# A hybrid transformer step on one core: attention logits as three rounded products, and heads 4 to 7 turned at other places

## The chip, the core and the metric

The kernel runs on one core of a Trainium2 chip. The metric is the device time of one execution in microseconds (us); lower is better. Several engines work beside one another, each on its own list of instructions: TensorE (PE) multiplies matrices, VectorE (DVE) and ScalarE (ACT) do elementwise work, GpSimd (POOL) and SyncE (SP) mostly issue transfers. They wait for one another by semaphores.

## The reference

One sequence of 512 tokens goes through a state-space layer with a convolutional feed-forward layer, and an attention layer with a second feed-forward layer, all in float32. The change touches only the logits of the attention, and what prepares them. Cut to that:

```python
k, v = kv[..., :K_DIM].reshape(b, s, 8, 2, 64), kv[..., K_DIM:].reshape(b, s, 8, 128)
k = rms_norm(k, k_norm_g)                       # over the 64 of each map
q = rms_norm((rms_norm(x, ln_g) @ q_w).reshape(b, s, 8, 2, 64), q_norm_g)
logits = einsum('bqhcd,bkhcd->bhcqk', q, k) * 64 ** -0.5 + rel_bias[t5_bucket(dist)]
p = softmax(where(dist >= 0, logits, -inf))     # causal; c = 0, 1 are the two maps of a head
attn = p[:, :, 0] - lam * p[:, :, 1]
o = einsum('bhqk,bkhd->bqhd', attn, v)
x = x + (rms_norm(o, subln_g) * (1 - lam_init)).reshape(b, s, -1) @ out_w
```

There are 8 heads, each with two maps of 64 dimensions; the result of a head is the difference of the two maps' softmaxes times the values.

## The kernel before, in words

Tokens lie in NT = 4 blocks of 128. Large products (projections) are taken as three float32r ("rounded") products: each operand is split into a rounded high part and a rounded rest, and high x high, high x low and low x high are added up in a PSUM bank. The helpers write the rounded high part on ACT (`wh_`, `xgh`, `oh`) and the rest on DVE (`wl_`, `xgl`, `ol`).

**Keys and queries.** `qk("q0")` projects the queries of heads 0 to 3, `keys` all keys by a seven-product scheme (the sums named `ps_K`), while `qk("q1")` (queries of heads 4 to 7) is part of the filling work described below. `head_norm` normalises each map (DVE, L1361) and `turned` turns blocks of 128 x 128 with transposes on TensorE into a PSUM bank, four to a bank; ACT (L1375) copies a bank with the gain into `kT[0]`, `kT[1]`, `qT[0]` and `qT[1]`, float32 tiles of 128 rows (two maps of 64) x 4 heads x 512 tokens. The sums of the second keys (heads 4 to 7) are kept in `qT[1]`, which is not needed yet. Unturned raw sums of the key scheme lie in a tile `key_raw` of the pool `kc`, which is closed when the keys are done; the pool `units` then takes over its memory.

**Attention lines.** Each head is cut into three units by `PARTS`: the query blocks 0 and 1, block 2, block 3, so that a unit has 384, 384 or 512 key columns a map (blocks 0 and 1 have 128 and 256). For a unit `logits` (L1527) multiplies the two maps side by side, rows 0 to 63 and rows 64 to 127 of the tiles, into two PSUM banks; DVE adds the bias `tb` and takes the maximum (L1533), ACT takes the exponential (L1540), DVE weighs the two maps (L1550: `weigh`), TensorE turns the result (L1559, step `a`), ACT copies it (L1560), TensorE multiplies it with the values (L1570, step `v`), and a finished head is normalised and turned for the output projection (step `o`, L1592, split by L1596 and L1597). The bias tile `tb` of a head is loaded by SP in the first unit of the head (two buffers); its first memory lies in the pool `units`.

TensorE's instructions in this part run in the order of the program text, which is written by hand in `ORDER`: 12 lines that each begin with a step `L` (the logits of two units, that is, one of (0, 1), (2, next head's 0) or (1, 2)) and one line more. `f` is one step of filling work: a part of a projection of six matmuls (values `v0`, queries `q1`, values `v1`, then the output projection). The instructions of the other engines and the transfers are put in order by the framework's scheduler. PSUM has four banks for turned, logits and value tiles (`aux_bank`) and four for projections, each taken in rotation.

Of the kernel before, what the change touches and what calls it, by code (L numbers as in the profile page):

```python
# [18 lines left out]
P = 128  # L19
T = 512  # L20
# [22 lines left out]
def trunk_kernel(ctx: ExitStack, tc, x, ssm_ln_g, ssm_in_w, ssm_conv_w, ssm_conv_b, ssm_dt_bias,  # L43
# [1249 lines left out]
    with tc.tile_pool(name="att", bufs=1) as ap, ExitStack() as later:  # L1293
        rts = []
        late = []

        kT = [ap.tile([P, 4, T], F32, name="kT%d" % i) for i in range(2)]
        qT = [ap.tile([P, 4, T], F32, name="qT%d" % i) for i in range(2)]
        vt = [ap.tile([P, D], F32, name="vt%d" % b) for b in range(NT)]

        def key_load(t, j, i, c, **more):
# [51 lines left out]
            act.activation(s, t, AF.Square)  # L1353
            dve.reduce_sum(out[:, b, :], s.rearrange("p (a q) -> p a q", a=8), axis=AX.X)

        def head_norm(key, kn, ss, dst, gcol, where):
            rsqrt_act(ss, ap, key, [P, NT, 8], 64)
            def normed():
                for b in range(NT):
                    v = kn[b].rearrange("p (a q) -> p a q", a=8)  # L1360
                    dve.tensor_tensor(out=v, in0=v, in1=ss[:, b, :].unsqueeze(2).to_broadcast([P, 8, 64]),  # L1361
                                      op=ALU.mult)

            if key == "q1":
                late.append(((0, 3), normed))
            else:
                normed()

            def turned(bs):
                for b in bs:  # L1370
                    ps = aux_bank("kt%s_%d" % (key, b))
                    for h in range(4):
                        pe.transpose(ps[:, h * P:(h + 1) * P], kn[b][:, h * P:(h + 1) * P], ident)
                    v = ps.rearrange("p (h t) -> p h t", h=4)
                    act.activation(dst[:, :, b * P:(b + 1) * P], v if key[0] == "k" else v[:, :, ::-1],  # L1375
                                   AF.Copy, scale=c2[:, gcol:gcol + 1])

            for at, bs in zip(where, ((0, 1), (2, 3))):
                late.append((at, lambda bs=bs: turned(bs)))

        def head_sums(key):
            return ap.tile([P, NT, 8], F32, tag="qss", name="ss" + key, bufs=2)

        def qk(key, dst, gcol, where):
            kn, ss = [], head_sums(key)

            def evac(b, ps, rt):
                t = ap.tile([P, T], F32, tag="kn", name="kn%s_%d" % (key, b), bufs=4)
                act.activation(t, ps, AF.Copy, scale=rt[:, b:b + 1])
                squared(key, t, rt, ss, b)  # L1390
                kn.append(t)

            yield from proj(key, evac)
            head_norm(key, kn, ss, dst, gcol, where)

        def keys(kc):

# [2 lines left out]

            def first(i, b, ps):
                acc[i][b] = (ap.tile([P, T], F32, tag="kn", name="key%d_%d" % (i, b), bufs=4) if i
                             else qT[1][:, b, :])
                if ps is not None:
                    act.activation(acc[i][b], ps, AF.Copy)

# [23 lines left out]
            def finish(i, where):  # L1430
                key, ss = "k%d" % (1 - i), head_sums("k%d" % (1 - i))
                for b in range(NT):
                    act.activation(acc[i][b], acc[i][b], AF.Copy, scale=rts[0][:, b:b + 1])
                    squared(key, acc[i][b], rts[0], ss, b)
                head_norm(key, acc[i], ss, kT[1 - i], 48, where)

            for m in SEVEN[1]:
                pss = [(aux_bank if m in "127" else mm_bank)("ps_K%s_%d" % (m, b)) for b in range(2)]
# [34 lines left out]
                        add(acc[0][2 + b], ps, r_)  # L1473
                if m == "3":
                    finish(1, ((4, 0), (4, 2)))
            finish(0, ((0, 1), (0, 3)))

        def vproj(key, i):
            def evac(b, ps, rt):
# [3 lines left out]
        PARTS = ((0, 1), (2,), (3,))  # L1483
        ORDER = ("f f L f f f a f",
# [12 lines left out]
        fl = lambda a: a.rearrange("p a b -> p (a b)")  # L1497
# [1 line left out]
        class Unit:  # L1499
# [9 lines left out]
            def logits(self):  # L1509
                h, tag, st = self.h, self.tag, self.st  # L1510
                if self.part == 0:
                    st["tb"] = up.tile([P, T], F32, tag="tb", name="tb%d" % h, bufs=2)
                    sync.dma_start(st["tb"], bass.AP(tensor=bd.tensor, offset=h * NBIAS + 1, ap=[[1, P], [1, T]]))
                    st["sm"] = up.tile([P, NT, 2], F32, tag="sm", name="sm%d" % h, bufs=3)
                i2, h4 = h // 4, h % 4
                k = len(self.ii)
                mx = up.tile([P, k, 2], F32, tag="mx%d" % k, name="mx" + tag, bufs=3)
                self.sm = st["sm"][:, self.ii[0]:self.ii[-1] + 1, :]
                self.p = [up.tile([P, T], F32, tag="p%d" % m, name="lg%s_%d" % (tag, m), bufs=3)
                          for m in range(2)]  # L1520
                pss = [aux_bank("lg%s_%d" % (tag, m)) for m in range(2)]
                for j, i in enumerate(self.ii):
                    n = (i + 1) * P
                    c = slice(self.off[j], self.off[j] + n)
                    for m in range(2):
                        rows = slice(64 * m, 64 * (m + 1))
                        pe.matmul(pss[m][:, c], qT[i2][rows, h4, i * P:(i + 1) * P], kT[i2][rows, h4, :n],  # L1527
                                  start=True, stop=True)
                for j, i in enumerate(self.ii):
                    n = (i + 1) * P  # L1530
                    c = slice(self.off[j], self.off[j] + n)
                    for m in range(2):
                        dve.tensor_tensor_reduce(self.p[m][:, c], pss[m][:, c],  # L1533
                                                 st["tb"][:, (3 - i) * P:], 1.0, 3.0e38,
                                                 ALU.add, ALU.min, mx[:, j, m:m + 1])
                for j, i in enumerate(self.ii):
                    n = (i + 1) * P
                    for m in range(2):
                        v = self.p[m][:, self.off[j]:self.off[j] + n]
                        act.activation(v, v, AF.Exp, bias=mx[:, j, m:m + 1], scale=-1.0,  # L1540
                                       accum_out=self.sm[:, j, m:m + 1])
# [103 lines left out]
            run(rest)  # L1645

        with tc.manual_schedule(engines={mybir.EngineType.PE}):
            run(qk("q0", qT[0], 49, (("2", 1), ("5", 0))))
            with tc.tile_pool(name="keys", bufs=1) as kc:
                keys(kc)  # L1650
            op_ = later.enter_context(tc.tile_pool(name="att_o", bufs=1))
            up = later.enter_context(tc.tile_pool(name="units", bufs=1))
            fill = chain(vproj("v0", 0), qk("q1", qT[1], 49, ((2, 0), (2, 1))), vproj("v1", 1),
                         attn_out(0, None, range(KB)))
            us = []
            for h in range(AH):
                st = {}
                us += [Unit(h, part, st) for part in range(len(PARTS))]
            for _ in range(10):
                next(fill)  # L1660

            turned, valued = iter(us), iter(us)
            valued_heads, normed_heads = [], []

            def norm_heads():
                while valued_heads:
                    u = valued_heads.pop(0)
                    normed_out(u.h, u.st)
                    normed_heads.append(u)

            def values():
                u = next(valued)
                u.values()
                if u.part == len(PARTS) - 1:
                    valued_heads.append(u)
                    if os:
                        with tc.issue_after(state["ol"]):
                            norm_heads()
                    norm_heads()

            def head_out():
                u = normed_heads.pop(0)
                os.append(turned_out(u.h, u.st))

            steps = {"f": lambda: next(fill), "a": lambda: next(turned).turn(), "v": values, "o": head_out}
            pairs = iter(zip(us[::2], us[1::2]))
            for step in " ".join(ORDER).split():
                if step == "L":
                    pair = next(pairs)
                    for u in pair:  # L1690
                        u.logits()
                    for u in pair:
                        u.weigh()
                else:
                    steps[step]()
            assert next(fill, None) is None
            last_out(norm1)
# [38 lines left out]
```

## Time and profile before

| | us |
|---|---|
| median of 3 runs | 1317.28 (1316.26 to 1317.30) |
| the profiled execution, its own time | 1317.05 |
| its span | 1315.3 |
| keys, in the span | about 745 to 808 |
| attention lines 0 to 11 and the line behind | about 808 to 945 |

The granted clock was full throughout. Times in the profile's rows are microseconds from the start of the span; PE is TensorE's matmuls, PEld its loads of the stationary operand, SPq and POOLq are transfers as they are issued. Matmuls are pipelined: the duration of one includes the way through the array, and what it costs is the distance from its start to the next one's. A group "x12" counts instructions of the trace; a float32 matmul stands there as two, a rounded one as one.

### The profile page before, as it was taken

The page shows a single profiled execution, that of the slowest core. Times are in us where ns is not written, and L with a number is a line of the kernel's source. Part 1 is how long each engine was busy: PE and PEld are TensorE (multiplying, and loading weights), DVE is VectorE, ACT ScalarE, POOL GpSimd, SP SyncE. Part 2 cuts the span into 40 slices and gives each one's busy share as a digit, 9 for nine tenths or more (in the row PEclk, how much of TensorE's full clock was granted, in tenths as well). Part 3 has the DMA queues.
Part 4 walks back from the last instruction along what each step waited for, and adds up shares of the span by engine and source line. Part 5 has one row for each costly group of instructions (what it writes and reads, how often), then busy time and mean ns, then how long its engine had stood idle before and what let it go on. Part 6 is the DMA issues. An engine that isn't in the chain of part 4 may idle for free.

```text
span 1315.3 us, 18265 instructions
## 1 busy us (share of the span) xinstructions
PE 1307.8 (99%) x6771; PEld 1096.2 (83%) x6771; DVE 1073.1 (82%) x1774; ACT 713.8 (54%) x1156; POOL 176.8 (13%) x244
## 2 busy tenths in 40 slices
PE   9999999999999999999999999999999999999998
PEld 8878888888888988898889887777888888888887
DVE  7989878888888877876888878677777978887886
ACT  6696554743344445544556667676654444544452
POOL 5230200300021401020113210000020100010001
PEclk9999999999999999999999999999999999999999
DMA  7453433432234657673766754222224445443635
GB/s 210 150 162 88 150 101 109 138 95 87 82 96 138 124 142 203 180 161 113 216 168 145 192 128 120 73 65 66 64 80 160 98 118 186 103 96 112 192 64 128
DMA packets 202552, 167.84 MB, mean 128 GB/s; under 512 B 7580, under 2 KB 175904, under 8 KB 202464
## 3 DMA queue, kind: packets, MB, share of 16 engines
q1 hardware_dynamic: 176080, 124.93, 31.8%
q0 software_dynamic: 22928, 36.46, 14.7%
q10 hardware_dynamic: 3456, 5.30, 1.1%
q8 instruction: 53, 0.87, 0.3%
q14 instruction: 35, 0.29, 0.1%
HBM read 160.21 MB, written 6.44 MB: 127 GB/s over the span
## 4 chain that ended last, share of the span: by engine, by line
PE 98%; ACT 1%; DVE 1%; issue 0%; DVEq 0%
PE ps_g L209 6%; PE ps_u L210 6%; PE ps_g L210 6%; PE ps_u L209 6%; PE ps_u L208 6%; PE ps_g L208 6%; PE ps_in L208 5%; PE ps_in L210 5%; PE ps_in L209 5%; PE ps_s L1239 3%; PE ps_s L1244 3%; PE ps_s L1242 3%; PE ps_s L1146 3%; PE ps_s L1141 3%; PE ps_s L1144 3%; PE ps_o L209 2%
## 5 line engine op out<-in xcount | busy, mean ns | idle before, releaser
L208 PE MATMUL ps_u<-xgh,wh_u 128*128 128x512 f32 x352 | 137.4, 390 | 0.0
L209 PE MATMUL ps_g<-xgl,wh_g 128*128 128x512 f32 x352 | 137.2, 390 | 0.0
L208 PE MATMUL ps_g<-xgh,wh_g 128*128 128x512 f32 x352 | 137.0, 389 | 0.0
L210 PE MATMUL ps_u<-xgh,wl_u 128*128 128x512 f32 x352 | 137.0, 389 | 0.0
L210 PE MATMUL ps_g<-xgh,wl_g 128*128 128x512 f32 x352 | 137.0, 389 | 0.0
L209 PE MATMUL ps_u<-xgl,wh_u 128*128 128x512 f32 x352 | 136.9, 389 | 0.0
L208 PE MATMUL ps_in<-xgh,wh_in 128*128 128x512 f32 x304 | 122.9, 404 | 0.0
L210 PE MATMUL ps_in<-xgh,wl_in 128*128 128x512 f32 x304 | 119.7, 394 | 0.0
L209 PE MATMUL ps_in<-xgl,wh_in 128*128 128x512 f32 x304 | 119.2, 392 | 0.0
L209 PEld LDWEIGHTS ps_g<-xgl,wh_g 128*128 128x128 f32 x352 | 66.0, 188 | 14.3 <-DVE xgl L488 0.7
L1244 PE MATMUL ps_s<-sl,wh_s 128*128 128x256 f32 x308 | 77.5, 283 | 0.0
L1242 PE MATMUL ps_s<-sh,wh_s 128*128 128x256 f32 x308 | 77.5, 283 | 0.0
L210 PEld LDWEIGHTS ps_g<-xgh,wl_g 128*128 128x128 f32 x352 | 66.1, 188 | 13.7
L209 PEld LDWEIGHTS ps_u<-xgl,wh_u 128*128 128x128 f32 x352 | 66.1, 188 | 13.6
L210 PEld LDWEIGHTS ps_u<-xgh,wl_u 128*128 128x128 f32 x352 | 66.0, 188 | 13.7
L208 PEld LDWEIGHTS ps_g<-xgh,wh_g 128*128 128x128 f32 x352 | 66.1, 188 | 13.6
L208 PEld LDWEIGHTS ps_u<-xgh,wh_u 128*128 128x128 f32 x352 | 66.1, 188 | 13.6
L1126 ACT ACTIVATE sh<-vg 128x256 fp32r<-128x256 f32 (+1 forms) x44 | 23.1, 524 | 99.1 <-DVE vg L1276 99.1
L1052 POOL DMA_DIRECT2D wz<-in_ffn_down_w_dram x36 | 44.2, 1290 | 235.2 <-DVE wl_s L1080 163.1
L1272 ACT ACTIVATE vg<-vg 128x512 f32<-128x512 f32 x44 | 27.8, 632 | 78.4 <-DVE vg L1024 78.3
L1024 DVE SCALAR_TENSOR_TENSOR vg<-ug,cf,vg 128x511 f32<-128x511 f32 x88 | 65.8, 747 | 5.5 <-ACT vg L1022 4.1
L1024 DVE SCALAR_TENSOR_TENSOR vu<-uu,cf,vu 128x511 f32<-128x511 f32 x88 | 65.7, 747 | 2.8 <-ACT vu L1022 1.4
(425 smaller groups left out, 3465.0 us busy)
## 6 DMA issues: line engine op xcount, KB each, us to landing
wr_g<-in_ffn_up_w_dram SPq DMA_DIRECT2D x44, 512.0 KB, 3.9
wr_u<-in_ffn_up_w_dram SPq DMA_DIRECT2D x44, 512.0 KB, 3.9
wr_in<-in_ssm_in_w_dram SPq DMA_DIRECT2D x40, 512.0 KB, 3.9
wz<-in_ffn_down_w_dram POOLq DMA_DIRECT2D x27, 512.0 KB, 5.8
m<-cumd POOLq DMA_DIRECT2D x16, 512.0 KB, 4.7
wr_out<-in_ssm_out_w_dram SPq DMA_DIRECT2D x16, 512.0 KB, 3.5
wr_s<-in_ffn_down_w_dram SPq DMA_DIRECT2D x13, 512.0 KB, 3.9
xT<-in_ffn_down_w_dram SPq DMA_DIRECT2D x10, 512.0 KB, 7.2
```

Of the source, the lines that this page charges most:

```text
L208: pe.matmul(ps, wh, xh, start=start, stop=False)
L209: pe.matmul(ps, wh, xl, start=False, stop=False)
L210: return pe.matmul(ps, wl, xh, start=False, stop=stop).ins
L1024: dve.scalar_tensor_tensor(out=v[:, s:], in0=u[:, :T - s], scalar=col(2 - s), in1=v[:, s:], op0=ALU.mult, op1=ALU.add)
L1052: pool.dma_start(view(t, nq), source(p0, c, nq, j, i), accum_op=ALU.add)
L1141: pe.matmul(pss[b], h, ws[q][1][:, cols], start=False, stop=end and q == qs[-1], skip_group_check=more)
L1144: pe.matmul(pss[b], h, ws[q][0][:, cols], start=first and q == qs[0], stop=False, skip_group_check=more)
L1146: pe.matmul(pss[b], w, ws[q][0][:, cols], start=False, stop=False, skip_group_check=more)
L1239: pe.matmul(v[:, b], wl[:, q, cols], h, start=False, stop=q == nq - 1, skip_group_check=not opens or b > 0)
L1242: pe.matmul(v[:, b], wh[:, q, cols], h, start=opens and q + b == 0, stop=False, skip_group_check=not opens or b > 0)
L1244: pe.matmul(v[:, b], wh[:, q, cols], w, start=False, stop=False, skip_group_check=not opens or b > 0)
L1272: act.activation(ga, ga, AF.Silu)
```

## The change: what it does

The turned keys and queries are kept as a rounded high part and a rounded rest (`kT_hi`, `kT_lo`, `qT_hi`, `qT_lo`, room for four heads, so that heads 4 to 7 take the places of 0 to 3 when those are used up), and the logits of a map are three rounded products in place of one float32 product. `turn_head` turns one head into a bank; ACT writes the high part and DVE (a new operation, L1366 of the changed kernel) the rest, from the same bank. The heads 4 to 7 are turned by steps of their own in `ORDER` (`k4` to `k7`, `q4` to `q7`); before, all keys were turned within the key products and the `q1` projection, and the later queries in two pieces of the filling work. The sums of the second keys are kept in `key_raw`, and normalised into the right halves of the value tiles `vt`, which are free until the values of heads 4 to 7 are ready. In lines 4, 7 and 10 of `ORDER` (line 0 is the first) steps `v`, `o` and `f` are exchanged beside that.

```diff
-        kT = [ap.tile([P, 4, T], F32, name="kT%d" % i) for i in range(2)]
-        qT = [ap.tile([P, 4, T], F32, name="qT%d" % i) for i in range(2)]
+        turned_by = {n: [ap.tile([P, 4, T], F32R, name=n + "T_" + x) for x in ("hi", "lo")] for n in "kq"}
+        second = {}
...
+        def turn_head(kind, h, src):
+            ps = aux_bank("kt%s%d" % (kind, h))
+            for b in range(NT):
+                pe.transpose(ps[:, b * P:(b + 1) * P], src[b][:, h % 4 * P:(h % 4 + 1) * P], ident)
...
+            act.activation(hi, v, AF.Copy, scale=g)
+            dve.scalar_tensor_tensor(out=lo, in0=v, scalar=g, in1=hi.bitcast(F32), op0=ALU.mult, op1=ALU.subtract)
...
-                             else qT[1][:, b, :])
+                             else whole_sums[:, b // 2, 2 * (b % 2):2 * (b % 2) + 2].rearrange("p k t -> p (k t)"))
...
-                head_norm(key, acc[i], ss, kT[1 - i], 48, where)
+                head_norm(key, acc[i], ss, where, None if i else [v[:, T:] for v in vt])
...
         ORDER = ("f f L f f f a f",
                  "L f f a v f v f a f",
-                 "L f f a v f v f a f",
-                 "L f f a v f v f o a f",
-                 "L f f a v f v f o a f",
-                 "L f f a v f v a f",
-                 "L f f a v f v o a f",
-                 "L f f a f v f o a f",
-                 "L f f v a f v v a",
+                 "L f f k4 a v f v f a f",
+                 "L f f k5 a v f v f o a f",
+                 "L f f a v f f v o k6 a f",
+                 "L f f a v f q4 v a f",
+                 "L f f k7 a v f q5 v o a f",
+                 "L f f a f o q6 f v a f",
+                 "L f f q7 v a f v v a",
                  "L f f a v f v o a f",
-                 "L f f a v f v o a",
+                 "L f f a v o f v a",
                  "L f f a v f v a",
                  "f a v f o v")
...
-                    for m in range(2):
-                        rows = slice(64 * m, 64 * (m + 1))
-                        pe.matmul(pss[m][:, c], qT[i2][rows, h4, i * P:(i + 1) * P], kT[i2][rows, h4, :n],
-                                  start=True, stop=True)
+                    for z, (q, k) in enumerate(((qh, kh), (ql, kh), (qh, kl))):
+                        for m in range(2):
+                            rows = slice(64 * m, 64 * (m + 1))
+                            pe.matmul(pss[m][:, c], q[rows, h4, i * P:(i + 1) * P], k[rows, h4, :n],
+                                      start=z == 0, stop=z == 2)
```

Three places show it in the order of instructions. First TensorE in line 0, the logits of the first unit (`lg0_0_0` and `lg0_0_1` are the banks of its two maps). Before:

```order
L1527 MATMUL lg0_0_0_7622<-kT0_6903,qT0_6905 128x128
L1527 MATMUL lg0_0_1_7623<-kT0_6903,qT0_6905 128x128
L1527 MATMUL lg0_0_0_7622<-kT0_6903,qT0_6905 128x256
L1527 MATMUL lg0_0_1_7623<-kT0_6903,qT0_6905 128x256
L1527 MATMUL lg0_1_0_7639<-kT0_6903,qT0_6905 128x384
L1527 MATMUL lg0_1_1_7640<-kT0_6903,qT0_6905 128x384
```

and in the changed kernel, of which the first 10 of 18 rows are shown:

```order
L1536 MATMUL lg0_0_0_7630<-kT_hi_6903,qT_hi_6905 128x128
L1536 MATMUL lg0_0_1_7631<-kT_hi_6903,qT_hi_6905 128x128
L1536 MATMUL lg0_0_0_7630<-kT_hi_6903,qT_lo_6906 128x128
L1536 MATMUL lg0_0_1_7631<-kT_hi_6903,qT_lo_6906 128x128
L1536 MATMUL lg0_0_0_7630<-kT_lo_6904,qT_hi_6905 128x128
L1536 MATMUL lg0_0_1_7631<-kT_lo_6904,qT_hi_6905 128x128
L1536 MATMUL lg0_0_0_7630<-kT_hi_6903,qT_hi_6905 128x256
L1536 MATMUL lg0_0_1_7631<-kT_hi_6903,qT_hi_6905 128x256
L1536 MATMUL lg0_0_0_7630<-kT_hi_6903,qT_lo_6906 128x256
L1536 MATMUL lg0_0_1_7631<-kT_hi_6903,qT_lo_6906 128x256
```

Each product of a map became three, and the maps still alternate.

Second, SP's queue ahead of line 0, where `tb` is a bias tile and `wr_q`, `wr_v` are pieces of weights. Before:

```order
L140 DMA wr_q_0_7560<-in_q_w_dram 128x2x512
L1513 DMA tb_7616<-bd 128x512
L1513 DMA tb_7707<-bd 128x512
L140 DMA wr_q_2_7654<-in_q_w_dram 128x2x512
L140 DMA wr_q_4_7739<-in_q_w_dram 128x2x512
L140 DMA wr_q_6_7819<-in_q_w_dram 128x2x512
L140 DMA wr_v_0_7912<-in_kv_w_dram 128x2x512
```

In the changed kernel:

```order
L140 DMA wr_q_0_7564<-in_q_w_dram 128x2x512
L140 DMA wr_q_2_7674<-in_q_w_dram 128x2x512
L140 DMA wr_q_4_7771<-in_q_w_dram 128x2x512
L140 DMA wr_q_6_7827<-in_q_w_dram 128x2x512
L1520 DMA tb_7624<-bd 128x512
L1520 DMA tb_7731<-bd 128x512
L140 DMA wr_v_0_7935<-in_kv_w_dram 128x2x512
```

The first two bias loads moved behind three weight loads, and the first of them now waits for DVE's last operation on `key_raw` (the normalising of `vt3`).

Third, DVE ahead of line 0's first operation that reads a bias tile, the last row of each. Before:

```order
L174 SCALAR_TENSOR_TENSOR wl_q1_0_7563<-wr_q1_0_7560,c2_89,wh_q1_0_7562 128x512
L501 TENSOR_TENSOR rst_k1_7474<-ssk1_7456 128x32
L502 SCALAR_TENSOR_TENSOR rst_k1_7474<-rst_k1_7474,rsm_k1_7473 128x32
L503 SCALAR_TENSOR_TENSOR ssk1_7456<-rst_k1_7474,ssk1_7456 128x32
L1361 TENSOR_TENSOR qT1_6906<-qT1_6906,ssk1_7456 128x512 x4
L174 SCALAR_TENSOR_TENSOR wl_q1_2_7657<-wr_q1_2_7654,c2_89,wh_q1_2_7656 128x512
L1533 ISA lg0_0_0_7620,mx0_0_7619<-lg0_0_0_7622,tb0_7616 128x128
```

In the changed kernel, where `ktk0` to `ktk3` are the banks of the turned keys of heads 0 to 3:

```order
L501 TENSOR_TENSOR rst_k1_7478<-ssk1_7460 128x32
L1366 SCALAR_TENSOR_TENSOR kT_lo_6904<-ktk1_7585,c2_89,kT_hi_6903 128x512
L502 SCALAR_TENSOR_TENSOR rst_k1_7478<-rst_k1_7478,rsm_k1_7477 128x32
L503 SCALAR_TENSOR_TENSOR ssk1_7460<-rst_k1_7478,ssk1_7460 128x32
L1375 TENSOR_TENSOR vt0_6907<-key_raw_7106,ssk1_7460 128x512
L1375 TENSOR_TENSOR vt1_6908<-key_raw_7106,ssk1_7460 128x512
L1375 TENSOR_TENSOR vt2_6909<-key_raw_7106,ssk1_7460 128x512
L1375 TENSOR_TENSOR vt3_6910<-key_raw_7106,ssk1_7460 128x512
L1366 SCALAR_TENSOR_TENSOR kT_lo_6904<-ktk2_7604,c2_89,kT_hi_6903 128x512
L1366 SCALAR_TENSOR_TENSOR kT_lo_6904<-ktk3_7611,c2_89,kT_hi_6903 128x512
L174 SCALAR_TENSOR_TENSOR wl_q1_2_7677<-wr_q1_2_7674,c2_89,wh_q1_2_7676 128x512 x2
L1542 ISA lg0_0_0_7628,mx0_0_7627<-lg0_0_0_7630,tb0_7624 128x128
```

Low halves (L1366) of four heads came in (that of `ktk0` stands in the row above the first one shown), two of them ahead of the normalising, which now goes from `key_raw` to `vt`.

More of the change, by code (lines that the diff above doesn't have):

```diff
@@ L1354, in squared, with head_norm @@
             dve.reduce_sum(out[:, b, :], s.rearrange("p (a q) -> p a q", a=8), axis=AX.X)
-        def head_norm(key, kn, ss, dst, gcol, where):
+        def turn_head(kind, h, src):
+            ps = aux_bank("kt%s%d" % (kind, h))
+            for b in range(NT):
+                pe.transpose(ps[:, b * P:(b + 1) * P], src[b][:, h % 4 * P:(h % 4 + 1) * P], ident)
+            g = c2[:, 48:49] if kind == "k" else c2[:, 49:50]
+            v, hi, lo = (t.rearrange("p (b t) -> p b t", b=NT) for t in [ps] + [t[:, h % 4] for t in turned_by[kind]])
+            if kind == "q":
+                v = v[:, :, ::-1]
+            act.activation(hi, v, AF.Copy, scale=g)
+            dve.scalar_tensor_tensor(out=lo, in0=v, scalar=g, in1=hi.bitcast(F32), op0=ALU.mult, op1=ALU.subtract)
+        def head_norm(key, kn, ss, where, to=None):
             rsqrt_act(ss, ap, key, [P, NT, 8], 64)
+            to = to or kn
             def normed():
                 for b in range(NT):
-                    v = kn[b].rearrange("p (a q) -> p a q", a=8)
-                    dve.tensor_tensor(out=v, in0=v, in1=ss[:, b, :].unsqueeze(2).to_broadcast([P, 8, 64]),
+                    v, o = (t[b].rearrange("p (a q) -> p a q", a=8) for t in (kn, to))
+                    dve.tensor_tensor(out=o, in0=v, in1=ss[:, b, :].unsqueeze(2).to_broadcast([P, 8, 64]),
                                       op=ALU.mult)
@@ L1367, in head_norm, with qk @@
                 normed()
[L1369 to L1379, printed above, removed]
+            if key[1] == "1":
+                second[key[0]] = to
+                return
+            for at, hs in zip(where, ((0, 1), (2, 3))):
+                late.append((at, lambda hs=hs: [turn_head(key[0], h, to) for h in hs]))
         def head_sums(key):
             return ap.tile([P, NT, 8], F32, tag="qss", name="ss" + key, bufs=2)
-        def qk(key, dst, gcol, where):
+        def qk(key, where=()):
             kn, ss = [], head_sums(key)
@@ L1393, in qk @@
             yield from proj(key, evac)
-            head_norm(key, kn, ss, dst, gcol, where)
+            head_norm(key, kn, ss, where)
         def keys(kc):
@@ L1475, in keys @@
                     finish(1, ((4, 0), (4, 2)))
-            finish(0, ((0, 1), (0, 3)))
+            finish(0, ())
         def vproj(key, i):
@@ L1514, in logits @@
                     st["sm"] = up.tile([P, NT, 2], F32, tag="sm", name="sm%d" % h, bufs=3)
-                i2, h4 = h // 4, h % 4
+                (kh, kl), (qh, ql) = (turned_by[n] for n in "kq")
+                h4 = h % 4
                 k = len(self.ii)
@@ L1647, in trunk_kernel @@
         with tc.manual_schedule(engines={mybir.EngineType.PE}):
-            run(qk("q0", qT[0], 49, (("2", 1), ("5", 0))))
+            run(qk("q0", (("2", 1), ("5", 0))))
             with tc.tile_pool(name="keys", bufs=1) as kc:
@@ L1652, in trunk_kernel @@
             up = later.enter_context(tc.tile_pool(name="units", bufs=1))
-            fill = chain(vproj("v0", 0), qk("q1", qT[1], 49, ((2, 0), (2, 1))), vproj("v1", 1),
+            fill = chain(vproj("v0", 0), qk("q1"), vproj("v1", 1),
                          attn_out(0, None, range(KB)))
@@ L1693, in trunk_kernel @@
                         u.weigh()
+                elif step[0] in "kq":
+                    turn_head(step[0], int(step[1]), second[step[0]])
                 else:
```

## The prediction

> **What bounds the kernel.** I read the page first, then the busy time of each stage, then the stretch of TensorE's timeline around each logits block, and last what ended TensorE's few pauses.
>
> ```profile
> span 1315.3 us, 18265 instructions
> PE 1307.8 (99%) x6771; PEld 1096.2 (83%) x6771; DVE 1073.1 (82%) x1774; ACT 713.8 (54%) x1156; POOL 176.8 (13%) x244
> PE 98%; ACT 1%; DVE 1%; issue 0%; DVEq 0%
> 745.00:808.00 63.00, 63.00 (x295) 52.50 (x294) 49.43 (x83) 43.53 (x69) 7.28 (x7) 1.00 0.67 150
> 808.00:931.00 123.00, 120.63 (x687) 93.62 (x686) 90.22 (x294) 90.25 (x240) 0.00 (x0) 1.00 0.21 65
> 931.00:965.00 34.00, 34.00 (x171) 28.03 (x170) 25.75 (x39) 19.45 (x35) 8.22 (x6) 1.00 0.28 78
> ```
>
> The chain that ended last is 98% TensorE, and in the three stretches that the change touches (keys, attention lines, tail; columns: length, then busy time of PE, PEld, DVE, ACT, POOL, then clock) TensorE is idle for 2.37 us only, all of it in 808 to 931. DVE has 13.6 and 32.8 us free in the first two. So a change here pays in two ways alone: less TensorE work, or a TensorE wait gained or lost.
>
> **Logits on TensorE.** These rows carry that term (start, duration, idle before in brackets):
>
> ```profile
> 699.86 0.28 PE L1242 MATMUL ps_s<-sh,wh_s 128*128 128x256 f32 x1
> 699.98 0.28 PE L1244 MATMUL ps_s<-sl,wh_s 128*128 128x256 f32 x1
> ...
> 808.81 1.57 PE L1527 MATMUL lg<-kT,qT 64*128 64x128 f32 x12
> 810.31 0.50 PE L1335 MATMUL ps_v<-wh_v,xgh 128*128 128x512 f32 x1
> ...
> 811.13 0.40 PE L1335 MATMUL ps_v<-wh_v,xgh 128*128 128x512 f32 x1
> 811.36 0.40 PE L1336 MATMUL ps_v<-wl_v,xgh 128*128 128x512 f32 x1
> ...
> 816.40 1.78 PE L1527 MATMUL lg<-kT,qT 64*128 64x512 f32 x12
> 818.11 0.51 PE L1335 MATMUL ps_q<-wh_q,xgh 128*128 128x512 f32 x1
> ...
> 829.06 1.77 PE L1527 MATMUL lg<-kT,qT 64*128 64x384 f32 x8
> 830.77 0.50 PE L1335 MATMUL ps_q<-wh_q,xgh 128*128 128x512 f32 x1
> ```
>
> Matmuls overlap, so a cost is the distance between starts, not a duration. A block with 768 columns a map (128, 256, 384) takes 810.31 - 808.81 = 1.50 us, one with 896 columns (512, 128, 256, or 384, 512) 1.71. The 0.21 for 128 more columns, in two passes, is 0.82 ns a column and pass; both maps share it, because the two run on different halves of the rows. 768 columns in two passes are 1.26, so 0.24 of a block is fixed. The rounded products now beside them cost 0.23 for 512 columns (811.36 - 811.13) and 0.12 for 256 (699.98 - 699.86): half as much a column, and 0.01 for each instruction; for 384 that gives 0.175. Three products instead of two passes at half the price are three quarters of the time. For 128 columns no rounded matmul stands in the trace. The line through the two others gives 0.065, a stationary operand of 128 columns may set 0.11:
>
> ```profile
> 862.52 0.60 PE L1592 MATMUL oT<-ident,ot 128*128 128x128 f32 x4
> 862.96 0.27 PE L1559 MATMUL at<-ident,lg 128*128 128x128 f32 x1
> ```
>
> (four transposes in 0.44). I take 0.11, since each of these too loads 128 columns for 128 moved. Then, per block, 3 x (0.11 + 0.12 + 0.175) + 0.24 = 1.455 against 1.50; 3 x (0.23 + 0.11 + 0.12) + 0.24 = 1.62 against 1.71; 3 x (0.175 + 0.23) + 0.24 = 1.455 against 1.71. Four of each: -1.6 us. With 0.065 it is -2.6; rows rounded to 0.01 leave some 0.3 either way. I take **-1.8**. If 128 columns cost as much as 512 (0.23), the result is about +1.3.
>
> A rule speaks against this term. The Trainium skill ("TensorE: Matmul & The Clock Gate", Part 3: Packing small matmuls) says that a weight load runs beside matmuls in flight only where its row group differs; the three products of one map all load into the same half. By that rule each load would lie bare. The trace is against it: the second pass of each matmul of before also loads the half that the first is using, and the 1.71 us of the block with 384 and 512 columns are 1.47 of streaming and 0.24 for everything else, where four bare loads would want 0.44.
>
> **What DVE, ACT and the banks gain.** The 64 transposes of keys and queries and the 16 ACT evacuations stay, in other groups (one head a bank). New are 16 DVE products (the low halves), reading PSUM; the nearest row is the same operation from PSUM, L1597:
>
> ```profile
> L1597 DVE SCALAR_TENSOR_TENSOR ol<-oT,c,oh 128x512 fp32r<-128x512 f32 x8 | 6.0, 747 | 5.1 <-ACT oh L1596 5.1
> ```
>
> 16 x 0.75 = 12.0 us: 8 of them (6.0) in the first stretch against 13.6 free, 8 in the second against 32.8 free. DVE does not become the bound; cost by itself nothing. But a bank of a turned head now comes free after the low half, 0.75 later. Eight such bursts (heads 4 to 7) stand at new places in lines 2 to 8. If TensorE waited out each low half, 6.0; if DVE's free quarter hides all, 0. I take +0.8 for these and other small waits (the likeliest: line 6's first products with a low half, which follow its burst closely, and line 4, where a second burst comes right behind an output), nearer to nothing because in the order most users of such a bank stand behind a projection step of six matmuls, 1.38 us.
>
> **Line 0 and the first bias load.** The second keys' sums move into the key pool's raw tile, whose memory the units' pool takes over. So the load of the first bias (tb) has to wait for the last normalising operation on it, and stands on SP's queue behind three weight loads. Before, it was long there:
>
> ```profile
> 792.87 0.81 SPq L1513 DMA_DIRECT2D tb<-bd  x2
> 794.82 9.89 SPq L140 DMA_DIRECT2D wr_q<-in_q_w_dram  x3
> ...
> DMA to landing us min/median/max: 3.0/4.0/4.8
> ...
> 803.56 0.75 DVE L174 SCALAR_TENSOR_TENSOR wl_q<-wr_q,c,wh_q 128x512 fp32r<-128x512 f32 x1
> 805.01 0.19 DVE L501 TENSOR_TENSOR rst_k<-ssk 128x32 f32<-128x32 f32 x1 [0.70 <-ACT ssk L500]
> ...
> 805.69 2.50 DVE L1361 TENSOR_TENSOR qT<-qT,ssk 128x512 f32<-128x512 f32 x4
> ...
> 810.35 0.28 DVE L1533 CUSTOM_DVE_ANT_0 lg<-lg,tb 128x128 f32<-128x128 f32 x1
> ...
> 812.65 0.73 DVE L174 SCALAR_TENSOR_TENSOR wl_q<-wr_q,c,wh_q 128x512 fp32r<-128x512 f32 x1
> ...
> 813.55 0.75 DVE L1550 SCALAR_TENSOR_TENSOR lg<-lg,sm,lg 128x128 f32<-128x128 f32 x2
> ...
> 814.58 0.49 PE L1559 MATMUL at<-ident,lg 128*128 128x128 f32 x3
> ```
>
> Two low halves go ahead of the normalising: one in the 0.70 idle, one (0.66 back to back) pushing it from 805.69 to 806.35, so it ends at 808.85. The three weight loads are issued by 804.7, so tb goes out at 808.85 and lands 3.0 to 4.0 later, 811.85 to 812.85. DVE has meanwhile two more low halves and two weight splits (2.7 us) and is ready at 811.5; so the load ends last. From the first bias row to the end of the weighing were 814.30 - 810.35 = 3.95, of them 0.65 a weight split that now stands ahead: 3.3. The transposes of line 0 can start at 815.15 to 816.15 instead of 814.58: **+1.1**, with line 0's own logits in it (and a half microsecond in which its third and fourth bank wait for low halves lies beside it). SP waits at tb with only later weight loads behind it, the next issued at 813.44 before.
>
> **Lines 4 and 7.** The 2.37 us of idle are two waits of the value products on ACT:
>
> ```profile
> 860.35 0.94 PE L1570 MATMUL po<-vt,at 128*128 128x128 f32 x6 [1.72 <-ACT at L1560]
> ...
> 893.92 0.49 PE L1570 MATMUL po<-vt,at 128*128 128x128 f32 x2 [0.65 <-ACT vt L1480]
> ```
>
> In line 4 one projection step (six matmuls of 0.23 = 1.38) now comes before that product: between 0 (if ACT comes as much later) and -1.7; by itself 0.34 would be left. I take -1.1, since TensorE also comes some 0.3 earlier by what the logits of four lines save, and ACT does not. In line 7 the product comes after an output, a turned head and a projection step (0.44 + 0.44 + 1.38), far more than 0.65: -0.65, or nothing if the next value column is late instead.
>
> **Sum.** -1.8 + 1.1 - 1.1 - 0.65 + 0.8 = -1.65. The profiled execution took 1317.05 (span 1315.3 and 1.75 around it), 0.23 under the median of 1317.28. That gives 1315.4, against the median -0.14%. 0.2% (2.6 us, 1314.65 to 1319.9) is about what a measurement here tells from no change.
>
> **Rivals.**
> - *All the favourable ends*: 128 columns at 0.065 (-2.6), tb in 3.0 us (+0.6), both stalls gone (-2.3), hardly a new wait (+0.2): -4.1, 1312.9. For it speaks that the median load was measured beside weight loads that will have landed; against it that line 4's ACT work is in a strict order that the change makes no shorter. 0.24.
> - *The rounded products of the two maps do not share the array.* Slower. A head's six products per width would cost 6 x (0.11 + 0.12 + 0.175 + 0.23) = 3.8 against 2 x 1280 x 0.82 ns = 2.1, so +13.7 in all, and 1315.4 + 1.8 + 13.7 = 1330.9. No rounded 64-row matmul stands in the trace; for sharing speaks that the plain ones share on the same rows. It decides once some three tenths of the sharing are lost (4.5 of 15.5 us). 0.04.
> - *Each weight load lies bare*, 0.11 on 12 pairs of products a head: 8 x 12 x 0.11 = +10.6, 1326. Against it stand the 0.24 fixed in a block of four load pairs. 0.03. (This is what the rule of the Trainium skill named above would do here.)
> - *Low halves become the wait*: banks late at most of the eight bursts, +5 in place of +0.8, or line 4's and 7's waits come back elsewhere: 1319.6 to 1321. DVE at 96 of 123 us speaks against, the strict order of DVE behind ACT for it. 0.13.
> - *128 columns cost like 512*: +1.3 for -1.8, 1318.5; the same. 0.09.
>
> The forecast itself (1314 to 1317) has 0.47; about 0.15 of that lies below 1314.65. Faster 0.24 + 0.15 = 0.39, slower 0.04 + 0.03 + 0.11 = 0.18 (part of the fourth stays within), same 0.43. The range 1311.3 to 1320.2 leaves out the second and third rivals, the end of the fourth and the luckiest of the first.
>
> **What would show it.** Right: logits blocks of about 1.45, 1.6 and 1.45 us with starts of the two maps a few ns apart; tb issued near 808.9 and a pause of some 1 us before line 0's transposes; no pause above 0.5 in lines 4 and 7. Wrong: 128-column steps far from 0.11; pauses of TensorE named by low halves; maps starting one behind the other.

## The result, and the profile after

The changed kernel takes 1315.37 us (median of 22 runs, 1314.3 to 1316.65), the kernel before 1316.91 (22 runs, 1316.21 to 1318.55); the ratio is 0.9987, with a 95% interval of 0.9981 to 0.9993. That is a small gain, clear of zero and inside the 0.2% that the prediction set as its bound, at the predicted 1315.4. Whether the terms of the sum were right is another matter, and the trace answers it better than the times.

The page and the two first stretches of the busy table, after:

```profile
span 1314.3 us, 18407 instructions
PE 1308.0 (100%) x6835; PEld 1100.5 (84%) x6835; DVE 1082.1 (82%) x1790; ACT 713.0 (54%) x1156; POOL 176.4 (13%) x244
PE 96%; DVE 2%; ACT 1%; issue 0%; DMA 0%; DVEq 0%
745.00:808.00 63.00, 63.00 (x296) 52.47 (x295) 52.78 (x89) 43.12 (x68) 7.97 (x7) 1.00 0.64 142
808.00:931.00 123.00, 122.15 (x765) 99.40 (x764) 100.42 (x307) 91.02 (x244) 0.00 (x0) 1.00 0.23 70
```

TensorE's visible idle time in 808 to 931 went from 2.37 to 0.85 us, and DVE's work rose by some 10. DVE's share of the chain went from 1% to 2%: TensorE waits for it where it did not before.

The part of the program ahead of the change scatters: the first query product starts between 727.5 and 728.9 us in the twelve traces of this study. So kernels are compared over the stretch R that the change touches, from the start of the last key product (`ps_K`) to that of the last output projection matmul (`ps_ao`). Before (the four `ps_K` start 0.23 apart, the last at 790.36):

```profile
789.68 1.07 PE L1446 MATMUL ps_K<-wl_K,xgh 128*128 128x512 f32 x4
...
962.13 0.39 PE L210 MATMUL ps_ao<-oh,wl_ao 128*128 128x512 f32 x1
```

After (the last at 790.76):

```profile
790.08 1.07 PE L1453 MATMUL ps_K<-wl_K,xgh 128*128 128x512 f32 x4
...
960.51 0.39 PE L210 MATMUL ps_ao<-oh,wl_ao 128*128 128x512 f32 x1
```

R is 171.77 before and 169.75 after: -2.02 us. Each R is from one trace. Single executions of one kernel differ by up to 2.4 us, but inside the traces the blocks repeat: the logits of line 1 take 1.58 or 1.59 in all eight kernels with rounded products. Differences in R of some tenths are therefore traced to the places where they arise; the times alone do not carry them.

The logits, undisturbed (line 2 after; "x2" are the two maps):

```profile
828.54 0.44 PE L1536 MATMUL lg<-kT_hi,qT_hi 64*128 64x384 f32 x2
828.82 0.34 PE L1536 MATMUL lg<-kT_hi,qT_lo 64*128 64x384 f32 x2
829.00 0.34 PE L1536 MATMUL lg<-kT_lo,qT_hi 64*128 64x384 f32 x2
829.17 0.41 PE L1536 MATMUL lg<-kT_hi,qT_hi 64*128 64x512 f32 x2
829.40 0.41 PE L1536 MATMUL lg<-kT_hi,qT_lo 64*128 64x512 f32 x2
829.63 0.40 PE L1536 MATMUL lg<-kT_lo,qT_hi 64*128 64x512 f32 x2
829.97 0.50 PE L1335 MATMUL ps_q<-wh_q,xgh 128*128 128x512 f32 x1
```

Both maps go in 0.23 us for 512 columns, and the block takes 1.43 instead of 1.70. The other two kinds take 1.41 (839.76 to 841.17) instead of 1.50, and 1.58 (817.72 to 819.30) instead of 1.71. Four of each save 4 x (0.27 + 0.09 + 0.13) = 2.0 us, as much as the whole change of R.

And yet the twelve blocks together, from the start of each to the matmul behind it, take 19.99 after and 20.31 before. Three blocks are long. Line 5 after:

```profile
864.37 0.34 PE L1536 MATMUL lg<-kT_lo,qT_hi 64*128 64x384 f32 x2
864.76 0.50 PE L1536 MATMUL lg<-kT_hi,qT_hi 64*128 64x512 f32 x1
865.42 0.50 PE L1536 MATMUL lg<-kT_hi,qT_hi 64*128 64x512 f32 x1 [0.16 <-DVE kT_lo L1366]
865.42 0.72 PE L1536 MATMUL lg<-kT_hi,qT_lo 64*128 64x512 f32 x2
865.76 0.62 PE L1536 MATMUL lg<-kT_lo,qT_hi 64*128 64x512 f32 x2
866.31 0.50 PE L1335 MATMUL ps_v<-wh_v,xgh 128*128 128x512 f32 x1
```

and what DVE did there:

```profile
863.96 0.74 DVE L1606 SCALAR_TENSOR_TENSOR ol<-oT,c,oh 128x512 fp32r<-128x512 f32 x1
864.62 0.74 DVE L1366 SCALAR_TENSOR_TENSOR kT_lo<-ktk,c,kT_hi 128x512 fp32r<-128x512 f32 x1
```

The first map's bank comes free with the split of the turned output (864.70), the second's with the low half of key head 6 (865.36). The maps fall out of step, "x2" becomes "x1" and "x1", and the block takes 2.40 instead of 1.43. A bracket shows 0.16 of it: the wait hides behind matmuls that still drain, so it is read from the distance of starts. Line 0 lost 0.59 in its block in the same way, to the second of two low halves that DVE ends at 810.44. Line 8 lost 0.39, but not to a low half: its second bank comes free when ACT has copied the turned result of line 7 (L1569, to 897.41), and the first product into it starts at 897.47.

### The profile page after: what moved, and what is told of

The parts are those of the page before. It is cut to its first block, busy times and chain, and to the rows that moved or that the text cites. A ratio compares the mean times of both kernels' runs of the same rounds, so it can differ in the third digit from the quotient of the medians.

```text
span 1314.3 us, 18407 instructions
## 1 busy us (share of the span) xinstructions
PE 1308.0 (100%) x6835; PEld 1100.5 (84%) x6835; DVE 1082.1 (82%) x1790; ACT 713.0 (54%) x1156; POOL 176.4 (13%) x244
## 4 chain that ended last, share of the span: by engine, by line
PE 96%; DVE 2%; ACT 1%; issue 0%; DMA 0%; DVEq 0%
PE ps_g L210 6%; PE ps_u L208 6%; PE ps_g L209 6%; PE ps_g L208 6%; PE ps_u L210 6%; PE ps_u L209 6%; PE ps_in L208 5%; PE ps_in L210 5%; PE ps_in L209 5%; PE ps_s L1239 3%; PE ps_s L1244 3%; PE ps_s L1242 3%; PE ps_s L1144 3%; PE ps_s L1146 3%; PE ps_s L1141 3%; PE ps_o L209 2%
```

## The experiments

Ten kernels, each timed against the kernel before; of one (map by map) there is a single execution. R is in us.

| kernel | R | ratio of times to before (95%) |
|---|---|---|
| before | 171.77 | |
| changed | 169.75 | 0.9987 (0.9981 to 0.9993) |
| changed, float32 logits | 169.53 | 0.9983 (0.9975 to 0.9992) |
| changed, old places in lines 4, 7, 10 | 171.31 | 0.9996 (0.9987 to 1.0005) |
| changed, early bias | 169.28 | 0.9982 (0.9974 to 0.9991) |
| changed, key head 6 in line 5 | 169.59 | 0.9980 (0.9971 to 0.9989) |
| before, new places in lines 4, 7, 10 | 169.38 | 0.9983 (0.9974 to 0.9992) |
| changed, map by map | 169.97 | one time, 1314.67 us |
| changed, two moves | 168.94 | 0.9981 (0.9972 to 0.9990) |
| changed, four moves | 167.83 | 0.9971 (0.9960 to 0.9983) |
| four moves, float32 logits | 168.72 | 0.9977 (0.9968 to 0.9986) |
| four moves, map by map | 167.64 | 0.9964 (0.9951 to 0.9978) |

**The float32 product back, all else as changed.**

```diff
-                    for z, (q, k) in enumerate(((qh, kh), (ql, kh), (qh, kl))):
+                    for z, (q, k) in enumerate(((qh, kh),)):
```

(with float32 tiles, and without the low halves).

> The changed kernel's storage, turning steps and ORDER, but the logits as one float32 product again and no low halves. The stretch R, from the last key product (ps_K) to the last output projection matmul (ps_ao), is 171.77 us in the kernel before and 169.75 in the changed one. Theory A (the account of the prediction: products -2.0, places in ORDER about -1.95, paid back by late banks and the late bias about +2): the undisturbed logits blocks are 1.50, 1.71 and 1.70 again (+2.0), but the banks come free 0.75 us earlier and the waits in lines 0, 5 and 8 (0.6, 1.0, 0.4 in the changed kernel) mostly go, so R is 169.6 to 170.8. Rival B (the products bring nothing, the gain is all from the places): R is as much shorter as the low halves' waits cost, about 168. Rival C (the products bring all, the places nothing): R is 171.5 or more.

Measured: R is 169.53, just under the range, and **0.22 shorter than with the rounded products**. The block that was long in line 5:

```profile
863.88 1.77 PE L1535 MATMUL lg<-kT_hi,qT_hi 64*128 64x384 f32 x8
865.58 0.50 PE L1335 MATMUL ps_v<-wh_v,xgh 128*128 128x512 f32 x1
```

takes its plain 1.70: nobody waits for a low half. In the changed kernel the rounded products save 2.0 us of TensorE work and cost as much in waits for what they need. Their net worth is about nothing; the 0.22 is too small for the times to confirm, whose intervals overlap.

**The old places in lines 4, 7 and 10.**

```diff
-                 "L f f a v f f v o k6 a f",
+                 "L f f a v f v f o k6 a f",
...
-                 "L f f a f o q6 f v a f",
+                 "L f f a f v f o q6 a f",
...
-                 "L f f a v o f v a",
+                 "L f f a v f v o a",
```

> The changed kernel with the steps v, f and o of lines 4, 7 and 10 in the order of before (the turning steps stay). Theory A: the waits of 1.3 and 0.65 us before the value products of lines 4 and 7 come back, R is 171.7 (171.0 to 172.2) instead of 169.75. Rival B (all from the places): the same. Rival C (places nothing): 169.5 to 170.2, the waits turn up elsewhere or are covered by the new turning steps.

```profile
860.13 0.60 PE L1579 MATMUL po<-vt,at 128*128 128x128 f32 x3 [1.74 <-ACT at L1569]
...
893.33 0.49 PE L1579 MATMUL po<-vt,at 128*128 128x128 f32 x2 [0.80 <-ACT vt L1487]
```

Both waits are back, as theory A and rival B said alike, and R is 171.31; rival C is out. It is only 1.56 longer, not 1.95. Read from the starts of the logits blocks, line 4 costs 1.41 more and line 7 1.04, and line 11's logits lose 0.43; but the logits of lines 5 and 8 no longer wait their 0.97 and 0.39 (line 5 goes from 865.09 to 866.52, 1.43): a TensorE that comes 1.3 later finds its banks free.

**The new places alone, in the kernel before.**

```diff
-                 "L f f a v f v f o a f",
+                 "L f f a v f f v o a f",
...
-                 "L f f a f v f o a f",
+                 "L f f a f o f v a f",
...
-                 "L f f a v f v o a",
+                 "L f f a v o f v a",
```

> The kernel before with the steps v, f and o of lines 4, 7 and 10 in the new order, nothing else (float32 logits, heads 4 to 7 turned in the old places). R (last ps_K to last ps_ao) is 171.77 in the kernel before, 169.75 in the changed one, 169.53 in the changed one with float32 logits. Theory A' (after the float32 run: the gain is that of the places, and what the products save is paid back in waits of their low halves): the waits of 1.72 and 0.65 us in lines 4 and 7 shrink as in the changed kernel, R is 169.8 (169.5 to 170.3). Rival (the places gain only together with the new turning steps, which fill the room): 171.0 or more.

R is 169.38, just below the range: **three lines of the list give 2.39 us, as much as the whole change or a little more** (the intervals of the times overlap). Line 4's wait, and line 11's logits before and here:

```profile
859.87 0.82 PE L1570 MATMUL po<-vt,at 128*128 128x128 f32 x5 [0.35 <-ACT at L1560]
...
923.03 1.92 PE L1527 MATMUL lg<-kT,qT 64*128 64x384 f32 x8
924.88 0.50 PE L208 MATMUL ps_ao<-oh,wh_ao 128*128 128x512 f32 x1
```

```profile
925.58 2.32 PE L1527 MATMUL lg<-kT,qT 64*128 64x384 f32 x8
927.83 0.50 PE L208 MATMUL ps_ao<-oh,wh_ao 128*128 128x512 f32 x1
```

The second fence is before. The parts are 1.72 - 0.35 = 1.37 in line 4, 0.65 in line 7, and 2.25 - 1.85 = 0.40 in line 11, which line 10's move gave; their sum is 2.42.

**The first bias load early.**

```diff
-                    st["tb"] = up.tile([P, T], F32, tag="tb", name="tb%d" % h, bufs=2)
+                    st["tb"] = (ap.tile([P, T], F32, tag="ksq", name="tb0", bufs=1) if h == 0 else
+                                up.tile([P, T], F32, tag="tb", name="tb%d" % h, bufs=2))
```

> The changed kernel with the first head's bias tile in another place (a work tile that is free from 803 to 858), so that its load waits for nothing late and is issued some 4 us earlier. Theory A: DVE starts the bias rows 0.7 us earlier, TensorE no longer waits before the transposes of line 0 (0.42), while the 0.6 in which the third and fourth logits bank wait for low halves stays: R is 169.3 (169.1 to 169.5). Rival D (the load is not what ends last; the low halves in front of the bias rows are): R stays within 0.15 of 169.75.

In the changed kernel SP issued the load at 809.19, and DVE waited for it:

```profile
809.19 0.81 SPq L1520 DMA_DIRECT2D tb<-bd  x2
```

```profile
810.35 1.41 DVE L174 SCALAR_TENSOR_TENSOR wl_q<-wr_q,c,wh_q 128x512 fp32r<-128x512 f32 x2
812.47 0.29 DVE L1542 CUSTOM_DVE_ANT_0 lg<-lg,tb 128x128 f32<-128x128 f32 x1 [0.71 <-DMA tb<-bd]
```

In this run it goes out at 803.21, DVE goes on without a break, and R is 169.28, as expected to 0.02.

**Key head 6 turned later**, in line 5 instead of behind line 4's output step.

```diff
-                 "L f f a v f f v o k6 a f",
-                 "L f f a v f q4 v a f",
+                 "L f f a v f f v o a f",
+                 "L f f k6 a v f q4 v a f",
```

> The changed kernel with the turning of key head 6 moved from line 4, right behind the output step, to line 5 behind the first two filling steps. Theory A: the wait of 0.97 us in the logits of line 5, whose fourth bank waits for that head's low half, goes: R is 168.8 (168.6 to 169.2). Rival E (the ACT and DVE work in front of it is late as a whole, and the next bank in the rotation waits in its place): R stays within 0.3 of 169.75.

Theory A missed and rival E holds. R is 169.59, and line 5 waits for the next bank in the rotation, that of the turned output:

```profile
864.02 0.39 PE L1536 MATMUL lg<-kT_hi,qT_hi 64*128 64x512 f32 x1
864.66 0.49 PE L1536 MATMUL lg<-kT_hi,qT_hi 64*128 64x512 f32 x1 [0.25 <-DVE ol L1606]
```

Its split stood behind the normalising of the later queries on DVE (862.05 to 863.86). Moving one burst off a late engine uncovered the next one.

**Map by map instead of alternating.**

```diff
-                    for z, (q, k) in enumerate(((qh, kh), (ql, kh), (qh, kl))):
-                        for m in range(2):
+                    for m in range(2):
+                        for z, (q, k) in enumerate(((qh, kh), (ql, kh), (qh, kl))):
```

> The changed kernel with the order of the loops over products and maps exchanged: the three products of one map, then the three of the other, so that neighbours use the same half of the rows. Same products, same result. Theory (the maps share the array, and that is what the term of -2.0 rests on): the products stand one behind the other, an undisturbed block of 768 columns goes from 1.41 to some 2.6 us and one with 384 and 512 from 1.43 to 2.6, R grows by 13 us (10 to 15). Rival (sharing needs no alternation, the two halves run ahead of each other): R within 1 us of 169.75. If loads of the same half lie bare, each of the products costs 0.1 more and R grows by 17 or more.

The theory missed by far: R is 169.97. The rival is right, and no load lies bare:

```profile
817.03 0.51 PE L1536 MATMUL lg<-kT_hi,qT_hi 64*128 64x512 f32 x2
817.37 0.39 PE L1536 MATMUL lg<-kT_hi,qT_lo 64*128 64x512 f32 x2
817.60 0.39 PE L1536 MATMUL lg<-kT_lo,qT_hi 64*128 64x512 f32 x2
```

The program has three products of one map, then three of the other; the trace has them in pairs of the same kind, the second map's first product 0.01 us behind the first map's.

**Two moves**: the output step of line 4 ahead of the second value step, where TensorE was idle for 0.41, and key head 6 in line 5.

```diff
-                 "L f f a v f f v o k6 a f",
-                 "L f f a v f q4 v a f",
+                 "L f f a v f f o v a f",
+                 "L f f k6 a v f q4 v a f",
```

> The changed kernel with the output step of line 4 ahead of its second value step, where TensorE sat idle for 0.41, and key head 6 turned in line 5 behind the first two filling steps. Theory F (line 5's 0.97 us is a wait for two banks in a row, first the split of the turned output, then the low half; each alone leaves the other, as the run with the key alone moved left 0.8): both go, and the idle of 0.41 is filled: R is 168.5 (168.2 to 168.9). Rival E (ACT's and DVE's work in front is late as a whole): 169.3 to 169.8.

R is 168.94, between the two. The idle of 0.41 is gone, and the wait in line 5 fell from 0.97 to 0.61 but stayed.

**Four moves**: these two, the early bias, and key heads 2 and 3 turned in line 1.

```diff
-                 "L f f a v f v f a f",
+                 "L f f k2 a v f k3 v f a f",
```

> The run before this one, with the early bias load, and with key heads 2 and 3 turned by steps in line 1 instead of just ahead of line 0. Theory A': line 0 loses its wait of 0.6 for the low halves of these two heads as well as the 0.4 at its transposes: R is 167.4 (167.1 to 168.0), and the time 1313 us. Rival (two more turned heads in line 1 make a new wait there, or in line 2): 168.0 to 168.8.

R is 167.83 and the time 1313.19 us. Line 0's block is undisturbed (807.13 to 808.54, 1.41), nothing new waits in lines 1 and 2; it is 0.43 above the expected 167.4, as the two moves alone were 0.44 above theirs: line 5 still takes 2.03 instead of 1.43. The trace shows on whom it waits. The turned output of line 4 is split by ACT and then by DVE:

```profile
859.07 0.67 ACT L1608 ACTIVATE oh<-oT,c 128x512 fp32r<-128x512 f32 x1
...
859.88 1.29 DVE L1375 TENSOR_TENSOR knq<-knq,ssq 128x512 f32<-128x512 f32 x2
861.09 0.75 DVE L1609 SCALAR_TENSOR_TENSOR ol<-oT,c,oh 128x512 fp32r<-128x512 f32 x1
```

ACT is ready at 859.74, but DVE first normalises two blocks of the later queries, so the bank comes free at 861.84, and the second map's first product starts at 861.89. No run moved that normalising.

**The same with float32 logits** (the edit of the first experiment).

> The kernel with all four moves (output step first in line 4, key head 6 in line 5, key heads 2 and 3 in line 1, early bias load), but with one float32 product for the logits and no low halves. With the rounded products it had R = 167.83. Theory A'' (the products are worth their 2 us once nobody waits for the low halves; in that kernel 1.0 us of waits is left in the logits of lines 5 and 8): undisturbed blocks 1.50, 1.71 and 1.70 again, R is 168.8 (168.4 to 169.1). Rival (the products save nothing net even there, as in the changed kernel): R is 167.5 to 168.0.

R is 168.72, as expected. So once most of the low halves are out of the way, the rounded products are worth 0.89 us; the waits left in lines 5 and 8, neither of which is for a low half, take the rest of their 2.0.

**The four moves, map by map.**

> The kernel with all four moves, and the three products of one map ahead of the three of the other. In the changed kernel with that order the logits of line 8 took 1.54 us instead of 1.82, as the first map's products no longer stand behind a second bank that comes late; line 5 gained nothing. Theory G (that is the order's doing): line 8 takes 1.55, R is 167.5 (167.2 to 167.7) against 167.83. Rival (line 8 differed by chance of ACT's order): R within 0.15 of 167.83.

R is 167.64, as expected, and the time 1312.35 us, the best of this study. Line 8 takes 1.57 instead of 1.84. But the traces do not show that the order did it. ACT's copy that frees line 8's second bank, and the products that wait for it, with the maps alternating and map by map:

```profile
893.74 0.61 ACT L1572 ACTIVATE at<-at 128x512 f32<-128x512 f32 x1
...
894.08 0.82 PE L1539 MATMUL lg<-kT_hi,qT_hi 64*128 64x512 f32 x2
...
895.29 0.50 PE L208 MATMUL ps_ao<-oh,wh_ao 128*128 128x512 f32 x1
```

```profile
894.08 0.62 ACT L1572 ACTIVATE at<-at 128x512 f32<-128x512 f32 x1
...
894.71 0.55 PE L1539 MATMUL lg<-kT_hi,qT_hi 64*128 64x512 f32 x2
...
895.65 0.49 PE L208 MATMUL ps_ao<-oh,wh_ao 128*128 128x512 f32 x1
```

In the first the bank comes free at 894.35, 0.27 after the other map's product has started (894.08); in the second at 894.70, just before that product starts (894.71). Counted from the start of the block, ACT's copy ends 0.28 earlier map by map (0.62 instead of 0.90), and in the kernels without the four moves 0.29 earlier. So the edit brought ACT's work forward, and what the order of the products itself is worth is not shown by line 8. Line 5 is the fair comparison, because there the bank comes equally late in both kernels, 1.08 and 1.06 behind the start of the block. It takes 2.03 with the maps alternating and 2.01 map by map:

```profile
861.99 0.39 PE L1539 MATMUL lg<-kT_hi,qT_hi 64*128 64x512 f32 x1
862.23 0.39 PE L1539 MATMUL lg<-kT_hi,qT_lo 64*128 64x512 f32 x1
862.46 0.38 PE L1539 MATMUL lg<-kT_lo,qT_hi 64*128 64x512 f32 x1
862.47 0.49 PE L1539 MATMUL lg<-kT_hi,qT_hi 64*128 64x512 f32 x1
862.81 0.39 PE L1539 MATMUL lg<-kT_hi,qT_lo 64*128 64x512 f32 x1
863.04 0.39 PE L1539 MATMUL lg<-kT_lo,qT_hi 64*128 64x512 f32 x1
863.36 0.50 PE L1335 MATMUL ps_v<-wh_v,xgh 128*128 128x512 f32 x1
```

Here the late bank did what the order alone did not: it parted the maps. The first two products of one map run by themselves, 0.23 apart; its third starts together with the other map's first, and that map's last two run by themselves again, 0.23 apart. A product alone costs as much as a pair.

## Why the prediction was right, point by point

- *Logits, -1.8*: the undisturbed blocks give -2.0. Products for 512 and 384 columns cost what the neighbours' rows said. For 128 columns the taken 0.11 holds for two of three products; the first takes 0.06 (818.52 to 818.58), and the first of 256 columns behind them 0.17 instead of 0.12 (818.81 to 818.98), so that the two together come to what was taken. What is left over in a block is 0.20 or 0.21 instead of 0.24.
- *Line 0, +1.1*: the load was issued at 809.19 (forecast 808.85) and ended last, as forecast. TensorE's second transpose started 1.27 later than before, and 0.40 of that it had brought along: +0.87. The half microsecond that was said to run beside it does: with the load early, R gains 0.47, and the other 0.59 stays in the logits block.
- *Lines 4 and 7, -1.1 and -0.65*: the idle went from 1.72 to 0.41 and from 0.65 to nothing.
- *Small waits, +0.8*: line 5 (0.97) and line 8 (0.39), 1.36 in all, so the term was too small. Line 5 had been named by the step that caused it, the second burst right behind line 4's output. The other place named, line 6, does not wait (1.41); line 8's wait is for an ACT copy.
- *Missing from the sum*: line 10's move. It has no term in the prediction, but line 11's logits waited 0.55 before and 0.23 after. The experiment on the places shows that the move is worth 0.4.

The sum of what was measured is -2.0 + 0.87 - 1.31 - 0.65 + 1.36 - 0.32 = -2.05, against -2.02 in R and -1.65 forecast. The ratio makes it 1.7 (0.9 to 2.5). That the time came within 0.03 us of the forecast is luck in part: four terms were off by 0.2 to 0.6 and a fifth was missing, with errors to both sides, and the median of the kernel before is 0.37 lower over 22 runs than over the three from which the forecast started. What holds is the kind and the sign of each term, and that a small gain is left of them.

What the sum could not show is which part brings the gain. It reads as if the products brought most of it. The runs say that the places alone bring 2.39 and the rest of the change, added to them, +0.37; on the old places the same rest brings -0.46 (171.31 against 171.77), which the times cannot tell from nothing. The two largest costs, in lines 0 and 5, belong to the same part as the -2.0: they are waits for its low halves and for memory that its storage holds, and in line 5 also for a split that DVE does late. A sum of terms gives the time; whether a part pays is seen only from the part alone, since every wait that is taken away brings TensorE earlier to the next one.

The rivals: the rows refute the 128-column price, the sharing rival and the bare loads. The Trainium skill's rule on bare loads (the title and section named above) is not borne out: three products in a row load the same half here at 0.23 us for 512 columns (861.99 to 862.46, the other half idle), the price of a full product beside them. The same section of the Trainium skill also names loads into a background weight buffer among those that are pulled ahead of matmuls; whether these loads are of that kind, no trace here shows. The rival on low halves had the right mechanism, at a third of the size given for it. Of the favourable ends none but the stall in line 7 came: line 4 kept 0.41, and line 0 cost 0.87.

The price of maps that do not share can be read from the parted block above: 0.23 for a product of 512 columns alone, as the sharing rival had it. Its condition did not come about, since undisturbed pairs take the same 0.23.

## What to carry to other kernels

When one engine is busy 99% of the time, as here, cheaper instructions on it pay only as far as their inputs and banks arrive as early: read for each new producer who holds the bank until when, and put it where a step's worth of other work lies between it and the bank's next user. Look for visible idle first: here three exchanged lines in the order of work gave more than the new arithmetic. And time a bundle's parts apart, because the trace of the whole cannot say which part paid.

## What the runs showed of the hardware that was not expected

Two matmuls on different halves of the rows need not stand next to each other to share the array. With three products of one map ahead of the other map's, the second map's first product started 0.01 us behind the first map's first (817.03 us, "x2"), ahead of two products that precede it in the program. The Trainium skill ("TensorE: Matmul & The Clock Gate", Part 3: Packing small matmuls) says that matmuls start and end in the order of the program; across halves of the rows this trace does not agree. Where one of two banks is late, neither order helps: the block of line 5 takes 2.03 us alternating and 2.01 map by map, with the bank equally late.
